# Low parts of every second piece of the output weights and last gate weights formed by an accumulating DMA instead of VectorE

## The chip, the cores and the metric

The kernel runs on one core of a Trainium2 chip. The metric is device time in microseconds (us) of one execution, from the start to the end of the program on that core. The engines of the core are TensorE (PE, with its weight loads PEld), VectorE (DVE), ScalarE (ACT), GpSimd (POOL) and SyncE (SP); each runs its own instructions in order and waits on semaphores of the others. DMA transfers are issued from the queues of SP, ACT and POOL and move data on 16 DMA engines that they share.

## What is computed

One block of a network over 256 rows of 2048 columns, in float32. The reference, cut to its frame:

```python
def reference(x, p, ...):
    h = x
    for l in range(DEPTH):                       # DEPTH is 1
        hn = rms_norm(h, ln_gain[l])
        z = split_columns(hn @ w_in[l] + b_in[l])
        y_a = rglru_branch(...) * silu(z['lru_gate'])
        y_b = nsa_branch(...) * silu(z['nsa_gate'])
        y_c = fox_branch(...) * silu(z['fox_gate'])
        mg = sigmoid(z['merge']).reshape(b, s, N_BRANCH, D_MODEL)
        merged = (mg[:, :, 0] * (y_a @ w_branch[l, 0])
                  + mg[:, :, 1] * (y_b @ w_branch[l, 1])
                  + mg[:, :, 2] * (y_c @ w_branch[l, 2]))
        h = h + merged @ w_out[l]                # "out"
        e = rms_norm(p[l] @ w_ple[l], ple_gain[l])
        h = h + sigmoid(h @ w_ple_gate[l]) * e   # "gate"
    return h
```

The change touches only the two last products, `merged @ w_out` and `h @ w_ple_gate`, each 256 x 2048 by 2048 x 2048.

## The kernel before

Every product is formed three times. An operand is cut into a high part, its rounding to float32r (a type that TensorE multiplies faster than float32), and a low part, the rest. With `hi`, `lo` of the activations and `wh`, `wl` of the weights, `mm3` adds hi x wh, hi x wl and lo x wh in PSUM.

All weights lie in one stream in HBM, in the order in which they are used, cut into 384 pieces. `plan()` lists the pieces. A full piece holds 128 rows x 1024 values, 512 KB. The stream ends with four chunks of kind "out" (512 columns each, 8 pieces each), three of kind "gate" (512 columns, 8 pieces each) and two of kind "gate" with 256 columns (4 pieces each): 64 pieces. I call the pieces of the second out chunk o1.0 to o1.7 (the chunks are o0 to o3), those of the gate chunks g0.0 and so on (g0 to g4). For each 512-column piece of these, `by_rows` issues 12 matmuls on PE: two row tiles, two blocks of 128 weight rows, three products; the first of a piece reads `wh`, the second `wl`.

The main loop is at piece i when it emits, in this order: the load of piece i + 5 on SP's queue (`issue`, tile `raw`, 4 buffers), the cut of piece i + 3 (`cut`), then what a new chunk needs (`before`), then the matmuls of piece i, then the end of the chunk, if it is its last piece. `cut` takes buffers `wh` and `wl` of rings of four. ACT writes `wh` as a copy of `raw` rounded to float32r, and DVE writes `wl = raw - wh`. As the ring has four buffers, `wh` of a piece waits until PE is through with the piece four places before.

`before` loads 512 KB from POOL's queue at the start of a chunk: `xc` (columns of x, for an out chunk) or `ec` (for a gate chunk, then also the 256 KB of `bias`, one buffer). Both `xc` and `ec` are tiles of the pool `k4`, a ring of five buffers of 4 KB a partition. DVE adds `xc` at the end of an out chunk (`k_h<-main,k_xc`); at the end of a gate chunk ACT takes a tanh of the sums (`k_fin<-main`), DVE multiplies it with `ec` (`k_fin<-k_fin,k_ec`) and adds h, and SP's queue stores it. After each out chunk the h just formed is turned by PE in two groups of four transposes (`bank<-cst,k_h`) among the first pieces of the next chunk. Side work beside the stream is over by the out chunks. Every operation passes a helper, so the profile gives one line, L191, for all of them.

Of the kernel before, what the change touches and what calls it, by code (L numbers as in the profile page):

```python
# [16 lines left out]
P = 128  # L17
# [5 lines left out]
EPS = 1e-6  # L23
# [17 lines left out]
# The small vectors, one column of 128 rows each.  # L41
# [8 lines left out]
# Constants of the shapes alone.  # L50
# [9 lines left out]
# Columns of the input projection whose products come out with rows on partitions, by chunk.  # L60
# [15 lines left out]
def plan():  # L76
    """The order of the weights: pieces of products, with what each needs and starts."""
# [53 lines left out]
    for c0, n in ((0, 512), (512, 512), (1024, 512), (1536, 256), (1792, 256)):  # L131
        out += item("gate", (c0, n), KT, n, ("w_ple_gate", None, [(c0, n)]), rows=1024 // n,
                    needs=lambda k: (f"ht{k // 4}",))
    at = 0
# [6 lines left out]
class Clock:  # L141
    """Estimates, in ns, of when each engine is through with what was emitted for it: an instruction
    starts once its engine is free and the last uses of its operands that matter to it are over."""
# [6 lines left out]
    def add(self, which, cost, out, ins, late=0.0):  # L150
        start = self.t[which]
        regions = [(out, True)] + [(x, False) for x in ins]
        spans = []
        for ap, writes in regions:
            free = list(ap.ap)[1:]
            lo = ap.offset
            hi = lo + sum(s * (n - 1) for s, n in free)
            name = ap.tensor.name
            # Two engines take turns at a bank of PSUM, whatever they do there.
            bank = name.startswith(("bank", "main"))  # L160
            if bank:
                lo, hi = 0, 1 << 30
            spans.append((name, lo, hi, writes))
            for l, h, t, w, e in self.uses.get(name, ()):
                if (writes or w or bank and e != which) and l <= hi and lo <= h:
                    start = max(start, t + (0.0 if e == which else 60.0))
        end = start + cost
        self.t[which] = end
        low = min(self.t[x] for x in ("pe", "v", "a"))
        for name, lo, hi, writes in spans:  # L170
            kept = [u for u in self.uses.get(name, ()) if u[2] > low and (bank or not writes or u[0] < lo or u[1] > hi)]
            self.uses[name] = kept + [(lo, hi, end + late, writes, which)]
# [8 lines left out]
class Metered:  # L181
    """An engine whose work is added to the clock."""
# [37 lines left out]
class Side:  # L220
    """Work beside the stream of weights, cut into steps that are dealt out along it."""
# [17 lines left out]
    def tick(self, hurry=False):  # L239
        """One step of every task that is under way, as long as the engines keep up."""  # L240
        while len(self.active) < self.most and self.pending:
            self.active.append(self.pending.popleft())
        for group in (self.urgent, self.active):
            for task in list(group):
                if self.clock.behind() > LIMITS[group is self.active] and not hurry:
                    return
                try:
                    if next(task[1]) and group is self.active:
                        group.remove(task)
                        group.append(task)  # L250
                except StopIteration:
                    self.done.add(task[0])
                    group.remove(task)
# [4 lines left out]
    def take(self, n=1):  # L258
        """n banks that are through with what was last in them."""
        while True:  # L260
            ready = [x for x in self.free if x[1] <= self.clock.t["pe"]]
            if len(ready) >= n:
                for x in ready[:n]:
                    self.free.remove(x)
                return [x[0] for x in ready[:n]]
            yield False
# [4 lines left out]
    def settle(self):  # L271
        """Until a product that reads what was emitted so far needn't wait for it."""
        t = self.clock.done()
        yield True
        while self.clock.t["pe"] < t:
            yield False

    def room(self, **need):
        """Room for a task's tiles."""
        while any(self.rooms[k] < n for k, n in need.items()):  # L280
            yield False
        self.give(**{k: -n for k, n in need.items()})
# [11 lines left out]
def block_kernel(ctx: ExitStack, tc: tile.TileContext, io):  # L294
# [44 lines left out]
    def splits(*parts):  # L339
        """Each source (times a scale) as the exact sum of two float32r tensors."""  # L340
# [16 lines left out]
    # ------------------------------------------------------------------ the stream of weights  # L357
# [4 lines left out]
    def issue(h, k=0, nk=None):  # L362
        """Loads a half's rows of 128, or nk of them from the k-th."""
# [7 lines left out]
    def cut(h, k=0, nk=None):  # L371
        m, n = h["nk"] * h["n"], h["n"]
        nk = nk or h["nk"]
        if k == 0:
            h["whl"] = [wp.tile([P, 1024], R32, tag=x, bufs=AHEAD + 1, name=nm(x)) for x in ("wh", "wl")]
        wh, wl = h["whl"]
        ks = slice(k * n, (k + nk) * n)
        split(wh[:, ks], wl[:, ks], h["raw"][:, ks])
# [5 lines left out]
    def by_rows(h, x):  # L384
        """Rows on partitions: two main banks, one of each row tile, gather the chunk's products."""
# [14 lines left out]
    def by_cols(h, x):  # L400
        """Columns on partitions: the chunk's column tiles in halves of main banks."""
# [14 lines left out]
    def banks_of(h):  # L416
        """The main banks of by_cols, each with its (first column tile, number of them)."""
# [7 lines left out]
    # ------------------------------------------------------------------ loads and constants  # L425
# [18 lines left out]
    # The causal mask of a tile, with none before and after.  # L444
# [13 lines left out]
    # Products of constants until the first weights are in: the array's clock rises with use.  # L458
# [3 lines left out]
    def rsqrt(out, ss, n):  # L462
        """out = (ss / n + EPS) ** -0.5"""
# [4 lines left out]
    def softplus(out, x, n):  # L468
        """out = max(x, 0) + log1p(exp(-|x|)), with log1p(u) = 2 atanh(u / (2 + u))"""
# [14 lines left out]
    def squares(x, acc, first):  # L484
        """acc += x^2, of two tiles"""
# [7 lines left out]
    def row_scales(name, acc):  # L493
        """(mean square of each of the 256 columns + EPS) ** -0.5, the same on all partitions."""
# [18 lines left out]
    # ------------------------------------------------------------------ operands kept on chip  # L513
# [13 lines left out]
    def hn_first(i, ks=range(2)):  # L527
        """Two tiles of x times its gain, as operands; the rows' scales come later."""
# [9 lines left out]
    def hn_again(i):  # L538
        """The same with the rows' scales."""
# [14 lines left out]
    # ---- p @ w_ple, normed, with its gain halved for the last gate  # L554
# [28 lines left out]
    # ---- gates: half of z (1 + tanh(z / 2)) is z sigmoid(z)  # L583
# [11 lines left out]
    # ---- RG-LRU, two tiles of 128 channels at a time  # L595
    def lru_task(i):
# [43 lines left out]
        # 1 - a^2 = tanh(-log a) (1 + a^2)  # L640
# [12 lines left out]
    # ---- keys and values of the sparse attention  # L653
    def unscaled(banks, dst, name, k0):
        """A chunk of the products without the rows' scales."""
# [9 lines left out]
    def cmp_task(banks):  # L665
        """The windows of 32 rows, with their positions added: 15 columns for each row and head."""
# [19 lines left out]
    def cmp_end():  # L686
# [6 lines left out]
        # The products with both parts of each block, added and turned.  # L693
# [31 lines left out]
    def norm_rows(z, n, dst):  # L725
        """dst(t) = z's groups of 128 columns, each row of a group normed."""
# [15 lines left out]
    def kk_task(z):  # L742
        # Of each head: window keys of row tiles 1 and 0, compressed keys, selected keys of tiles 0 and 1.
# [21 lines left out]
    # ---- sparse attention of a pair of heads and one row tile  # L765
    def nsa_task(g, pr, t):
# [18 lines left out]
        def soft(a, sc):  # L785
            """exp(score - maximum) and their sums: compressed, selected, window."""
# [71 lines left out]
    # ---- forgetting attention  # L858
    def forget_task():
# [10 lines left out]
        # lf holds softplus(-f) = -log f: the running sum is minus the cumulative log forget gate.  # L870
# [10 lines left out]
    def fox_task(h):  # L881
# [42 lines left out]
        # Key tile 0 of both row tiles, then key tile 1 of the second.  # L924
# [17 lines left out]
    # ---- branch outputs as operands  # L942
# [24 lines left out]
    def split_turned(name, dst, src, j, scale=None):  # L967
        """Columns 512 j .. of src, turned and split into dst."""
# [15 lines left out]
    # ------------------------------------------------------------------ the ends of chunks  # L984
# [49 lines left out]
    def read_by(name, gen):  # L1034
        """A task that reads the chunk's main banks."""
# [30 lines left out]
    def proj_chunk(h, out):  # L1066
        """merged += projection (1 + tanh): twice the gated sum, halved when it is split."""
# [33 lines left out]
    def before(h):  # L1101
        """What the end of a chunk asks for, loaded while its products are formed."""
# [14 lines left out]
    # ------------------------------------------------------------------ the program  # L1117
# [103 lines left out]
# The weights in flight; how many pieces are loaded and cut ahead.  # L1221
RAW, LOADS, AHEAD = 4, 5, 3
# Products of constants before the first weights.
WARM = 8
# Tiles of the pools that the tasks beside the stream may hold, and how many of them run at once.
ROOMS = dict(k1=7, k2=8, k4=5)
MOST = 3
# Nanoseconds: spared between an operand and its product; work that may wait on VectorE and ScalarE.
MARGIN = 1600.0
LIMITS = 3000.0, 2000.0  # L1230
# The first of p's products follows this chunk of the merge.
# [3 lines left out]
def stream(arrays):  # L1235
    """The weights, laid out one after the other as they are used."""
# [68 lines left out]
```

## Time and profile before

| | |
|---|---|
| median of three runs | 1110.47 us (1108.59 to 1111.84) |
| span of the profiled execution, first to last instruction | 1108.5 us |
| own time of the profiled execution | not listed apart; the lowest run stands 0.09 us above its span |
| PE busy | 1098.8 us, 99% of the span |
| DVE, ACT, POOL busy | 65%, 53%, 5% |
| moved by DMA | 220.88 MB, mean 199 GB/s |

Busy shares are means over the whole program. What a wait costs is read in the stretch in which it stands: the out and gate chunks fill the last 190 us or so of the span. Matmuls are pipelined, so one lasts longer in the profile (0.39 us) than the distance from it to the next (0.23 us).

### The profile page before, as it was taken

What the parts mean: (1) busy time and instruction counts of PE and PEld (TensorE: products, weight loads), DVE (VectorE), ACT (ScalarE), POOL (GpSimd) and SP (SyncE); (2) the same over time, 40 slices, a digit from 0 to 9 for tenths busy, and PEclk for the clock granted to TensorE, in tenths of its full rate; (3) what the DMA queues carried; (4) which work ended last, traced back from release to release, by engine and by line L of the source; (5) the groups of instructions that cost most, each with busy time, mean ns of one, the idle gap of its engine ahead of it and who ended that gap; (6) DMA issues with size and microseconds to landing.
All of it is one profiled execution on the core that took longest, in us unless ns stands there. A gap on an engine that the chain in (4) does not pass through costs nothing.

```text
span 1108.5 us, 16051 instructions
## 1 busy us (share of the span) xinstructions
PE 1098.8 (99%) x6123; PEld 957.4 (86%) x6123; DVE 725.9 (65%) x1108; ACT 588.2 (53%) x869; POOL 51.0 (5%) x70
## 2 busy tenths in 40 slices
PE   8999999999999999999999999999999999999998
PEld 8999998789988888888888888889888888888888
DVE  7679878877674765676776755554665565555554
ACT  7456786587654655454644544454554444444442
POOL 0100000010000000011010000000000100000000
PEclk9999999999999999999999999999999999999999
DMA  8656658756464554567557566766575775655773
GB/s 303 219 186 187 212 179 267 257 182 195 156 208 148 172 170 138 172 203 212 175 177 218 167 196 202 218 193 217 171 216 195 237 279 195 208 190 180 226 244 101
DMA packets 63293, 220.88 MB, mean 199 GB/s; under 512 B 7400, under 2 KB 8304, under 8 KB 63216
## 3 DMA queue, kind: packets, MB, share of 16 engines
q1 hardware_dynamic: 58176, 203.71, 55.6%
q0 software_dynamic: 4752, 15.76, 5.5%
q8 instruction: 48, 0.79, 0.3%
q10 hardware_dynamic: 288, 0.39, 0.1%
q14 instruction: 29, 0.24, 0.1%
HBM read 215.62 MB, written 4.20 MB: 198 GB/s over the span
## 4 chain that ended last, share of the span: by engine, by line
PE 97%; DMA 1%; DVE 1%; ACT 1%; issue 0%; DVEq 0%; ACTq 0%
PE main L191 90%; PE bank L191 7%; DMA raw<-in_w 1%; DVE wl L191 1%; ACT wh L191 0%; DMA k_xT<-in_xT 0%; ACT L191 0%; DVE k_fin L191 0%; DVE k_z L191 0%; ACT k_lru L191 0%; ACT k_hnh L191 0%; ACT k_fin L191 0%; DVEq L191 0%; ACTq L191 0%
## 5 line engine op out<-in xcount | busy, mean ns | idle before, releaser
L191 DVE TENSOR_TENSOR wl<-raw,wh 128x1024 fp32r<-128x1024 f32 (+3 forms) x385 | 463.8, 1211 | 320.2 <-ACT wh L191 319.1
L191 ACT ACTIVATE wh<-raw 128x1024 fp32r<-128x1024 f32 (+3 forms) x385 | 401.2, 1048 | 376.2 <-PE main L191 297.3
L191 PE MATMUL main<-wh,k_hnh 128*128 128x512 f32 (+1 forms) x736 | 285.0, 387 | 0.9 <-ACT wh L191 0.9
L191 PE MATMUL main<-wl,k_hnh 128*128 128x512 f32 (+1 forms) x736 | 281.3, 382 | 1.2 <-DVE wl L191 1.1
L191 PE MATMUL main<-wh,k_hnl 128*128 128x512 f32 (+1 forms) x736 | 281.0, 382 | 0.0
L191 PE MATMUL main<-k_hnh,wh 128*128 128x256 f32 x576 | 164.7, 286 | 1.5 <-ACT wh L191 1.5
L191 PE MATMUL main<-k_hnh,wl 128*128 128x256 f32 x576 | 164.1, 285 | 0.2 <-DVE wl L191 0.2
L191 PE MATMUL main<-k_hnl,wh 128*128 128x256 f32 x576 | 164.0, 285 | 0.0
L191 PEld LDWEIGHTS main<-wl,k_hnh 128*128 128x128 f32 x736 | 138.5, 188 | 26.7 <-DVE wl L191 2.6
L191 PEld LDWEIGHTS main<-wh,k_hnl 128*128 128x128 f32 x736 | 138.2, 188 | 26.7
L191 PEld LDWEIGHTS main<-wh,k_hnh 128*128 128x128 f32 x736 | 138.4, 188 | 26.3 <-ACT wh L191 1.2
L191 PEld LDWEIGHTS main<-k_hnh,wh 128*128 128x128 f32 x576 | 111.3, 193 | 2.0 <-ACT wh L191 1.8
L191 PEld LDWEIGHTS main<-k_hnh,wl 128*128 128x128 f32 x576 | 111.3, 193 | 0.5 <-DVE wl L191 0.4
L191 PEld LDWEIGHTS main<-k_hnl,wh 128*128 128x128 f32 x576 | 111.4, 193 | 0.1
L191 PE MATMUL main<-wh,k_yh 128*128 128x512 f32 x192 | 75.3, 392 | 0.0
L191 PE MATMUL main<-wh,k_yl 128*128 128x512 f32 x192 | 74.9, 390 | 0.0
L191 PE MATMUL main<-wl,k_yh 128*128 128x512 f32 x192 | 74.9, 390 | 0.0
L191 PE MATMUL main<-wh,k_hth 128*128 128x512 f32 (+1 forms) x160 | 55.7, 348 | 0.0
L191 PE MATMUL main<-wh,k_htl 128*128 128x512 f32 (+1 forms) x160 | 55.6, 347 | 0.0
L191 PE MATMUL main<-wl,k_hth 128*128 128x512 f32 (+1 forms) x160 | 55.5, 347 | 0.0
L191 PE MATMUL main<-wh,k_mth 128*128 128x512 f32 x128 | 50.7, 396 | 0.0
L191 PE MATMUL main<-wh,k_mtl 128*128 128x512 f32 x128 | 50.0, 391 | 0.0
(253 smaller groups left out, 1173.9 us busy)
## 6 DMA issues: line engine op xcount, KB each, us to landing
raw<-in_w SPq DMA_DIRECT2D x371, 512.0 KB, 4.1
bias<-in_b_in POOLq DMA_DIRECT2D x21, 256.0 KB, 4.3
raw<-in_w SPq DMA_DIRECT2D x8, 408.0 KB, 5.4
e_dram<-k_e POOLq DMA_DIRECT2D x4, 512.0 KB, 7.0
k_xc<-in_x POOLq DMA_DIRECT2D x4, 512.0 KB, 8.7
k_xT<-in_xT SPq DMA_DIRECT2D x7, 256.0 KB, 5.8
k_ec<-e_dram POOLq DMA_DIRECT2D x3, 512.0 KB, 7.8
out<-k_fin SPq DMA_DIRECT2D x6, 256.0 KB, 2.2
```

The lines of the kernel that those rows point to most:

```text
L191: r = call(out, *args, **kw)
```

## The change

Among the 64 pieces of the out and gate chunks every second one, from the 9th up to the 55th, is marked `summed`: pieces .0, .2, .4 and .6 of the chunks o1, o2, o3, g0, g1 and g2, 24 in all. For these the low part is formed otherwise. ACT writes the negated rounded weights into a tile `ws`, then a DMA from POOL's queue reads the same weights from HBM a second time and adds them to what stands in `ws`, so that `ws` holds weight minus high part. ACT then writes `wh` as before. DVE has nothing to do for these pieces. `ws` is not taken from the ring of `wl` but from the pool `k4`, which so far held `xc` and `ec` there.

```diff
@@ plan @@
+    last = [h for h in out if h["kind"] in ("out", "gate")]
+    for h in last[8:-8:2]:
+        h["summed"] = True
...
@@ cut @@
         if k == 0:
-            h["whl"] = [wp.tile([P, 1024], R32, tag=x, bufs=AHEAD + 1, name=nm(x)) for x in ("wh", "wl")]
+            h["whl"] = [wp.tile([P, 1024], R32, tag=x, bufs=AHEAD + 1, name=nm(x)) if x == "wh" or not h.get("summed")
+                        else mid([P, 1024], R32, name="ws") for x in ("wh", "wl")]
         wh, wl = h["whl"]
         ks = slice(k * n, (k + nk) * n)
-        split(wh[:, ks], wl[:, ks], h["raw"][:, ks])
+        if h.get("summed"):
+
+            A.activation(wl, h["raw"], AF.Copy, scale=-1.0)
+            G.dma_start(wl, bass.AP(tensor=wsrc.tensor, offset=wsrc.offset + h["off"], ap=[[m, P], [1, m]]),
+                        accum_op=OP.add)
+            A.activation(wh, h["raw"], AF.Copy)
+        else:
+            split(wh[:, ks], wl[:, ks], h["raw"][:, ks])
```

The rest of the diff takes comments out. The rows of PE and SP stand in the same order as before, but that PE reads `k_ws` in place of `wl`.

POOL's queue around the end of chunk g0 and the start of g1, before; a row is a DMA, written tile left of the arrow, `k_ec_9353` and `k_ec_9525` are the `ec` of g0 and g1:

```order
L191 DMA k_xc_9193<-in_x 128x2x512
L191 DMA k_ec_9353<-e_dram 128x2x512
L191 DMA bias_9355<-in_gain 128x512
L191 DMA k_ec_9525<-e_dram 128x2x512
L191 DMA bias_9527<-in_gain 128x512
```

The same place after the change; `k_ec_9367` and `k_ec_9543` are now the `ec` of g0 and g1:

```order
L194 DMA k_ec_9367<-e_dram 128x2x512
L194 DMA bias_9369<-in_gain 128x512
L194 DMA k_ws_9390<-in_w 128x1024
L194 DMA k_ws_9437<-in_w 128x1024
L194 DMA k_ws_9474<-in_w 128x1024
L194 DMA k_ws_9511<-in_w 128x1024
L194 DMA k_ec_9543<-e_dram 128x2x512
L194 DMA bias_9545<-in_gain 128x512
L194 DMA k_ws_9562<-in_w 128x1024
L194 DMA k_ws_9601<-in_w 128x1024
```

Between the `ec` of two chunks there are now four accumulating DMAs, so five tiles of `k4` after the `ec` of g0 comes that of g1, and takes its buffer. `k_ws_9562` is that of piece g1.4; it stands behind `ec` and `bias` of g1.

ACT at the same place before, from the end of g0; `wh_9521`, `wh_9543` and `wh_9561` are the high parts of g1.3, g1.4 and g1.5:

```order
L191 ACTIVATE k_fin_9509<-main_85 128x512
L191 ACTIVATE k_fin_9514<-main_86 128x512
L191 ACTIVATE wh_9521<-raw_9473 128x1024
L191 ACTIVATE wh_9543<-raw_9491 128x1024
L191 ACTIVATE wh_9561<-raw_9519 128x1024
```

ACT there after the change:

```order
L194 ACTIVATE k_fin_9527<-main_85 128x512
L194 ACTIVATE k_fin_9532<-main_86 128x512
L194 ACTIVATE wh_9539<-raw_9490 128x1024
L194 ACTIVATE k_ws_9562<-raw_9508 128x1024
L194 ACTIVATE wh_9561<-raw_9508 128x1024
L194 ACTIVATE wh_9580<-raw_9537 128x1024
L194 ACTIVATE k_ws_9601<-raw_9559 128x1024
```

The negated copy of g1.4, `k_ws_9562`, stands between the high parts of g1.3 and g1.4. It waits for no buffer of its own, but it stands behind `wh_9539`, which waits for PE.

## Rows read from the trace of the kernel before

**Rows 1.** The page, parts 1 and 4: busy time by engine, and the chain that ended last.

```profile
PE 1098.8 (99%) x6123; PEld 957.4 (86%) x6123; DVE 725.9 (65%) x1108; ACT 588.2 (53%) x869; POOL 51.0 (5%) x70
...
PE 97%; DMA 1%; DVE 1%; ACT 1%; issue 0%; DVEq 0%; ACTq 0%
```

**Rows 2.** The chain from 900 us on: start, duration, what.

```profile
972.33 0.44 PE bank L191 x4
...
975.54 0.44 PE bank L191 x4
...
1021.42 82.91 PE main L191 x456
1104.33 0.02 issue
1104.35 0.39 ACT k_fin L191
```

**Rows 3.** Groups of instructions from 880 us on: busy, mean ns, idle before.

```profile
L191 DVE TENSOR_TENSOR wl<-raw,wh 128x1024 fp32r<-128x1024 f32 x77 | 94.2, 1225 | 89.0 <-ACT wh L191 88.9
L191 ACT ACTIVATE wh<-raw 128x1024 fp32r<-128x1024 f32 x77 | 81.6, 1060 | 112.9 <-PE main L191 93.7 <-DMA raw<-in_w 18.6 <-ACT wh L191 0.7
```

**Rows 4.** Timeline of PE, one piece of o1: start, duration, instruction.

```profile
961.28 0.39 PE L191 MATMUL main<-wh,k_mth 128*128 128x512 f32 x1
961.51 0.39 PE L191 MATMUL main<-wl,k_mth 128*128 128x512 f32 x1
...
964.00 0.39 PE L191 MATMUL main<-wh,k_mth 128*128 128x512 f32 x1
```

**Rows 5.** Timeline of ACT: middle of o1, start of o2, start of g1.

```profile
961.48 1.06 ACT L191 ACTIVATE wh<-raw 128x1024 fp32r<-128x1024 f32 x1 [1.66 <-PE main L191]
...
969.64 1.06 ACT L191 ACTIVATE wh<-raw 128x1024 fp32r<-128x1024 f32 x1 [1.66 <-PE main L191]
...
1037.80 0.60 ACT L191 ACTIVATE k_fin<-main 128x512 f32<-128x512 f32 x1 [0.76 <-PE main L191]
1038.30 1.05 ACT L191 ACTIVATE wh<-raw 128x1024 fp32r<-128x1024 f32 x1
...
1046.22 1.06 ACT L191 ACTIVATE wh<-raw 128x1024 fp32r<-128x1024 f32 x1 [0.21 <-DMA raw<-in_w]
```

**Rows 6.** Timeline of DVE: end of o0, end of o1, end of g0.

```profile
948.02 1.23 DVE L191 TENSOR_TENSOR wl<-raw,wh 128x1024 fp32r<-128x1024 f32 x1 [0.30 <-ACT wh L191]
...
969.16 1.28 DVE L191 TENSOR_TENSOR k_h<-main,k_xc 128x512 f32<-128x512 f32 x2
...
1038.64 0.69 DVE L191 SCALAR_TENSOR_TENSOR k_fin<-k_fin,k_ec 128x512 f32<-128x512 f32 x1
```

**Rows 7.** Timeline of POOL: its DMAs from 881 us on.

```profile
881.35 2.85 POOL L191 DMA_DIRECT2D k_xc<-in_x  x4
884.20 0.70 POOL L191 DMA_DIRECT2D k_ec<-e_dram  x1
914.41 0.58 POOL L191 DMA_DIRECT2D bias<-in_gain  x1 [29.51 <-DVE k_mg L191]
948.02 0.71 POOL L191 DMA_DIRECT2D k_ec<-e_dram  x1 [33.03 <-DVE k_h L191]
```

**Rows 8.** Issue to landing: the k_ec of 948.02, the k_xc of 881.35, the k_ec of 884.20.

```profile
DMA to landing us min/median/max: 5.5/5.5/5.5
...
DMA to landing us min/median/max: 5.9/5.9/5.9
...
DMA to landing us min/median/max: 13.4/13.4/13.4
```

**Rows 9.** Issue to landing of raw, 940 to 1020 us (28 loads).

```profile
DMA to landing us min/median/max: 3.0/3.2/5.5
```

**Rows 10.** Stretches: busy time by engine, PEclk, DMA share, GB/s.

```profile
992.00:1015.00 23.00, 23.00 (x107) 19.05 (x106) 12.48 (x13) 9.46 (x10) 0.00 (x0) 1.00 0.54 184
1037.00:1060.00 23.00, 23.00 (x103) 19.07 (x102) 14.74 (x17) 10.06 (x12) 1.28 (x2) 1.00 0.69 229
```

**Rows 11.** GB/s from 880 to 1108.5 us in 40 slices of 5.71 us.

```profile
GB/s 217 354 404 269 188 199 224 209 165 180 201 206 268 162 199 202 211 136 204 212 192 147 211 192 194 143 278 112 268 290 319 73 263 253 318 122 255 69 3 46
```

## The prediction

> **What bounds the kernel now.** I read the page first: PE is busy for 99% of the span, and the chain that ended last runs on PE for 97% of it [rows 1]. Then I looked at the stretch that the change touches. The chain from 900 us on is PE alone: after the last group of transposes it is one run of 456 matmuls, 82.91 us, down to the first tanh after the last product [rows 2]. No wait of PE for `wl` or `wh` stands in it. PE takes a piece of 12 matmuls every 2.72 us (961.28 to 964.00), and reads `wl` in the second of them, 0.23 us into the piece [rows 4]. DVE and ACT are the ones that wait: DVE was idle for 89.0 us before its 77 subtractions, ACT for 112.9 us before its 77 copies, mostly for PE [rows 3]. The reader should see that what is taken from DVE here is taken from an engine that nobody waits for, and that the only thing the change can touch is the moment at which a low part is there.
>
> **What it removes and adds.** DVE loses 24 subtractions of 1.225 us, 29.4 us of work [rows 3]; worth nothing, since PE waited for none. ACT gains 24 copies of the same shape as `wh`, 1.06 us each, 25.4 us; in the out chunks it is busy 9.46 of 23.00 us [rows 10], and a pair of pieces (5.44 us) would hold three copies, 3.2 us. Hidden by the waits for PE; if they were gone it would cost as much as it lasts. POOL issues 24 DMAs of some 0.7 us [rows 7]; it does nothing else but six `xc` and `ec` and their biases. The raw buffer of a summed piece comes free at the end of ACT's copy and not of DVE's subtraction, some 1.2 us earlier, so SP's loads lose nothing by it. What remains is the transfer: 24 x 512 KB more from HBM, and as much read from SBUF to be added to.
>
> **The time that the transfer has, in the middle of a chunk.** Call S the start of piece j - 4 on PE. `wh` of j - 1 waits for the end of piece j - 5 and starts 0.20 us after S (961.48 against 961.28) [rows 4, 5]. It takes 1.06, the negated copy of j behind it 1.06: done at S + 2.32. PE wants `ws` at S + 4 x 2.72 + 0.23 = S + 11.11. So 8.8 us are left from issue to landing.
>
> **What the transfer takes.** The trace has no accumulating DMA, so I bound it. Below: a plain 512 KB from POOL's queue beside raw loads, 5.5 us [rows 8]. Above: the last of five such in a row, 13.4 us [rows 8]. The row of five also gives a pace: the first, issued at 881.35, landed 5.9 later, at 887.2; the fifth, issued at 884.20, at 897.6 [rows 7, 8]. That is 2.6 us for each further 512 KB when POOL's queue and SP's are both loaded. I count the accumulating one as two such shares, since it must fetch its target as well as its source: 5.5 + 2.6 = 8.1 us alone, and 5.2 behind another. I choose that over one share (it only copies) and over three because a second stream of the same size is the least that an addition in place needs. 8.1 is inside 8.8, and 5.2 inside the 5.44 of a pair, both narrowly: in the middle of a chunk I count no stall.
>
> The Trainium skill speaks here ("Collectives: The Full Stack", section "The bandwidth ceiling: the fold count and why AG ≠ RS ≠ AR"): an addition inside a DMA needs two source reads on the same ring and so runs at half the rate of a copy, measured as 62.28 against 32.35 GB/s. That would be 1.93 shares in place of two; by it the sum below would be some 8.3 us in place of 10.5 (0.36 less at each of six starts), and by the plain row alone nothing. No run here shows it.
>
> **At the start of a chunk** the transfer stands behind others. Now S is the start of the chunk on PE. The `ws` of piece .2 was issued at S - 5.44 + 2.32 and lands at S + 5.0. Behind it comes `xc` or `ec`, which now waits for the buffer of the chunk before: five tiles of `k4` earlier is the tile of that chunk. Before, all four `xc` and the first `ec` were issued by 884.9 [rows 7]. For o2, S is 969.44 (0.20 before the `wh` at 969.64), and DVE is through with `xc` at 970.44, S + 1.0 [rows 5, 6]. `xc` lands one share behind `ws`, at S + 7.6, and the `ws` of piece .4 two shares later, at S + 12.8. It is wanted at S + 11.11 + 0.88 (two groups of transposes [rows 2]) = S + 11.99. Late by 0.8 us; three times (o1, o2, o3), 2.4 us. For g1, S is 1037.60 (0.20 before the tanh at 1037.80), and DVE is through with `ec` at 1039.33, S + 1.7 [rows 5, 6]. `ec` lands at S + 7.6, 256 KB of `bias` at S + 8.9, the `ws` of g1.4 at S + 14.1; wanted at S + 11.11. Late by 3.0 us; g1 and g2, 6.0 us. g0 has the transposes too: 14.1 against 11.99, 2.1 us. What is late next: the `ws` of g1.6. In the trace of before the load of its `raw` came in at 1046.2 [rows 5], so its issue is at S + 9.7; it lands at S + 14.1 + 5.2 = 19.3, wanted at S + 16.55 + 3.0 = 19.55. In time. The DVE work that waits for `ec` holds back no low part that is needed before S + 16. Sum: 2.4 + 6.0 + 2.1 = **10.5 us**.
>
> The profile's span is 1108.5, the lowest run 0.1 above it; taking that as its own time, the sum is 1108.6 + 10.5 = 1119.1 for such an execution. The median of the runs stands 1.9 higher, and I give the time against it: 1110.47 + 10.5 = **1121.0 us**.
>
> **Rivals.** *In time everywhere (no change).* If the accumulating DMA costs what a copy does, it lands 5.5 us after its issue; at the start of g1 that is ec S + 7.2, bias S + 8.5, `ws` S + 11.1 against 11.11. PE never waits, and the time is 1110.5. For it: POOL's `ec` of 948.02 landed in 5.5 with raw loads beside it [rows 8], and the DMA engines are at 0.54 to 0.69 of their time here [rows 10]. Against: the target has to be read. It decides as soon as an accumulation costs under about half a share more. This is also the side on which nothing slower is seen; below it there is only the spread of the runs, since PE has no wait to lose.
>
> *DMA becomes the bound.* If an addition costs three shares, a pair of pieces moves five times 512 KB. The fullest slice of the trace moved 404 GB/s [rows 11], so 512 KB takes 1.30 us at best and the pair 6.5 against 5.44: 1.06 x 24 = 25 us, and six `xc` and `ec` with three biases another 7.5 x 1.30 = 9.8. Time 1145. For it: even with two shares the pair needs 5.2 of 5.44, so little is left; raw loads beside a full POOL queue would become late as well. Against: raw loads land in 3.2 us in the median [rows 9].
>
> *POOL held up by DVE.* If a subtraction on DVE kept POOL from issuing, each issue could come 1.2 us later: 8.1 + 1.2 = 9.3 against 8.8, 0.5 us for each of six transfers in mid-chunk, and 1.2 at each of six starts: 10.2 more, 1131. Against: the `ec` issued at 948.02 stood beside a subtraction that started at the same moment and took 1.23 us; the issue took 0.71, and its landing, 5.5, is the shortest of that size [rows 6 to 8]. The Trainium skill ("SBUF — State Buffer", section "Who interferes with whom") says that a DVE operation with two inputs in SBUF contends with GpSimd's reads, and one in a two-port mode locks GpSimd out altogether. By that row, the trace does not show it for this pair.
>
> **How the numbers follow.** Late at the starts of chunks, as summed: 0.45. In time everywhere: 0.26. DMA the bound: 0.25. POOL held up: 0.04. A measurement of this kernel tells some 0.3%, 3.3 us, from no change. The first, third and fourth are slower; the second is "same", but for 0.03 of luck below. A little of the first ends under 3.3 us, which gives faster 0.03, same 0.25, slower 0.72. The range reaches from the case in time, 1109.5, to just past the case in which DMA is the bound, 1146; the likeliest case's own range is 1114 to 1131 (an accumulation of 1.7 to 2.3 shares).
>
> **What would show it.** Of the changed kernel: a wait of PE for the DMA of `k_ws`, longest at the second matmul of g1.4 and g2.4 (about 3 us), under 1 us in the out chunks, none for `wh`; the landing of `k_ws` at 8 us in the middle of a chunk and 9 to 11 at its start; `ec` of g1 issued at 1.7 us after the chunk's start; DVE 29 us less busy, ACT 25 more. Landings of 5.5 to 7 would make the second case right, landings over 10 everywhere with raw loads late too the third. The prediction is wrong if PE waits in mid-chunk, or if nothing waits.

## The result and the profile after

The changed kernel takes 1125.04 us in the median of 4 runs (1122.58 to 1126.09), the kernel before 1110.18 us beside it: 14.9 us more, ratio 1.013 with a 95% interval of 1.0116 to 1.0144. The forecast was 1121.0, slower. The profiled execution has a span of 1123.1 us, 14.6 more than before.

The page of the changed kernel, part 1, then parts 3 and 6 in three rows (DMA queues with packets, MB, share of 16 engines; issues with KB each and us to landing):

```profile
PE 1105.4 (98%) x6123; PEld 960.5 (86%) x6123; DVE 698.3 (62%) x1084; ACT 611.7 (54%) x893; POOL 70.9 (6%) x94
...
q0 software_dynamic: 8208, 28.34, 11.3%
...
k_ws<-in_w POOLq DMA_DIRECT2D x24, 512.0 KB, 8.5
```

Against [rows 1], DVE is busy for 27.6 us less and ACT for 23.5 us more: the work went where the change sends it, and the end came later all the same.

The waits of PE from 930 us on (in total, times, longest); before, there was none [rows 2]:

```profile
PE main L194 <- DMA k_ws<-in_w: 8.9, 6, 3.8
```

Stretches of the changed kernel, one for each chunk o1, o2, o3, g0, g1, g2 from its first matmul to that of the next (columns as in [rows 10]: busy time by engine, PEclk, DMA share, GB/s):

```profile
946.24:969.98 23.74, 23.31 (x106) 18.67 (x104) 7.58 (x8) 13.36 (x14) 3.98 (x5) 1.00 1.02 292
969.98:993.10 23.12, 23.12 (x106) 18.61 (x104) 7.58 (x8) 13.47 (x14) 4.01 (x5) 1.00 1.00 291
993.10:1016.84 23.74, 23.32 (x105) 18.65 (x104) 7.58 (x8) 13.37 (x14) 4.55 (x6) 1.00 1.00 290
1016.84:1040.66 23.82, 23.35 (x105) 18.65 (x104) 8.83 (x10) 13.85 (x15) 4.63 (x6) 1.00 1.03 294
1040.66:1068.42 27.76, 23.83 (x98) 18.95 (x97) 8.85 (x11) 13.24 (x14) 4.60 (x6) 0.94 1.00 286
1068.42:1095.76 27.34, 23.53 (x98) 19.00 (x97) 10.86 (x13) 11.24 (x12) 3.65 (x5) 0.94 0.84 266
```

The second number is the length of the chunk. Before, the chunks o1 to g0 took 22.72 us each (the copies of `wh` that PE's end of a chunk released started at 946.92, 969.64, 992.36 and 1015.08) and g1 and g2 21.76. So the chunks are longer by 1.0, 0.4, 1.0, 1.1, 6.0 and 5.6 us, 15.1 in all, and three quarters of that lies in two of them. The other thing to see is the DMA share: 1.0, where it was 0.54 to 0.69 [rows 10], at under 300 GB/s, while the trace of before had a slice of 404 [rows 11]; only g2, with its long wait, has less, 0.84. In g1 and g2 the granted clock of PE is also lower.

The waits of PE in the out chunks and g0; the chunks o1, o3 and g0 start at 946.24, 993.10 and 1016.84:

```profile
958.88 0.50 PE L194 MATMUL main<-k_ws,k_mth 128*128 128x512 f32 x1 [0.43 <-DMA k_ws<-in_w]
993.88 0.50 PE L194 MATMUL main<-k_ws,k_mth 128*128 128x512 f32 x1 [0.40 <-DMA k_ws<-in_w]
1017.58 0.50 PE L194 MATMUL main<-k_ws,k_hth 128*128 128x512 f32 x1 [0.35 <-DMA k_ws<-in_w]
```

By their distance from the start of the chunk these are the second matmuls of o1.4, o3.0 and g0.0, each 0.5 to 0.6 us late.

The two stretches of g1 after its long wait, and PE's rows there:

```profile
1061.50:1066.00 4.50, 4.41 (x13) 3.52 (x14) 0.00 (x0) 1.11 (x2) 2.02 (x3) 0.64 1.05 289
1066.00:1080.00 14.00, 14.00 (x64) 11.58 (x63) 3.89 (x6) 6.29 (x8) 0.88 (x1) 1.00 0.95 276
```

```profile
1051.54 0.39 PE L194 MATMUL main<-wh,k_hth 128*128 128x512 f32 x1
1053.00 0.50 PE L194 MATMUL main<-k_ws,k_hth 128*128 128x512 f32 x1 [1.07 <-DMA k_ws<-in_w]
...
1061.60 0.80 PE L194 MATMUL main<-k_ws,k_hth 128*128 128x512 f32 x1 [2.86 <-DMA k_ws<-in_w]
1062.19 0.63 PE L194 MATMUL main<-wh,k_htl 128*128 128x512 f32 x1
1062.62 0.63 PE L194 MATMUL main<-wh,k_hth 128*128 128x512 f32 x1
```

The two that waited are the second matmuls of g1.4 and g1.6. The first came 1.2 us later than its place in the row (1053.00 against 1051.54 + 0.23), the other 3.0 us. After it the matmuls stand 0.43 us apart in place of 0.23 for six of them. In g2 nothing waits at g2.4, and g2.6 is late by 4.0 us:

```profile
1088.94 0.79 PE L194 MATMUL main<-k_ws,k_hth 128*128 128x512 f32 x1 [3.81 <-DMA k_ws<-in_w]
```

Why g1.6? The timeline of ACT in g1, and of POOL:

```profile
1050.65 1.06 ACT L194 ACTIVATE wh<-raw 128x1024 fp32r<-128x1024 f32 x1 [5.95 <-DMA raw<-in_w]
1053.53 1.06 ACT L194 ACTIVATE k_ws<-raw 128x1024 fp32r<-128x1024 f32 x1 [1.82 <-DMA raw<-in_w]
```

```profile
1037.73 0.84 POOL L194 DMA_DIRECT2D k_ws<-in_w  x1 [5.05 <-ACT k_ws L194]
1038.27 0.92 POOL L194 DMA_DIRECT2D k_ec<-e_dram  x1
1039.00 0.75 POOL L194 DMA_DIRECT2D bias<-in_gain  x1
1043.66 0.88 POOL L194 DMA_DIRECT2D k_ws<-in_w  x1 [3.91 <-ACT k_ws L194]
1054.89 0.86 POOL L194 DMA_DIRECT2D k_ws<-in_w  x1 [10.36 <-ACT k_ws L194]
```

ACT stood for 5.95 us before `wh` of g1.5 and 1.82 us before the negated copy of g1.6, both times for `raw`. On SP's queue the two stores of chunk g0 stand ahead of these loads:

```profile
1041.58 0.35 SPq L194 DMA_DIRECT2D out<-k_fin  x1
1042.94 0.34 SPq L194 DMA_DIRECT2D out<-k_fin  x1
1043.38 0.43 SPq L194 DMA_DIRECT2D raw<-in_w  x1
```

That order is the one of the kernel before, and the load of g1.5 starts no later in the chunk than it did (2.7 us after its start; 2.9 before). What grew is the time to landing: 7.2 us for g1.5, where it took 4.3, and 9.5 for g1.6, where it took 5.1. Before, ACT already waited at this place, without cost to PE:

```profile
1044.95 1.06 ACT L191 ACTIVATE wh<-raw 128x1024 fp32r<-128x1024 f32 x1 [3.37 <-DMA raw<-in_w]
```

So the accumulating DMA of g1.6 was issued at 1054.89, 14.2 us after the start of the chunk, and landed 6.7 us later, while PE wanted it at 1058.6. It was not this transfer that was slow, at 6.7 us against a median of 8.5, but its start that was late.

### The profile page after: what moved, and what is told of

The parts are those of the page before. It is cut to its first block, busy times and chain, and to the rows that moved or that the text cites. A ratio compares the mean times of both kernels' runs of the same rounds, so it can differ in the third digit from the quotient of the medians.

```text
span 1123.1 us, 16112 instructions
## 1 busy us (share of the span) xinstructions
PE 1105.4 (98%) x6123; PEld 960.5 (86%) x6123; DVE 698.3 (62%) x1084; ACT 611.7 (54%) x893; POOL 70.9 (6%) x94
## 4 chain that ended last, share of the span: by engine, by line
PE 86%; issue 6%; DMA 4%; ACT 1%; POOL 1%; DVE 1%; SPq 0%; POOLq 0%; ACTq 0%; DVEq 0%
PE main L194 80%; PE bank L194 6%; DMA k_ws<-in_w 3%; DMA raw<-in_w 1%; POOL k_ws L194 1%; ACT wh L194 1%; DVE wl L194 0%; ACT k_ws L194 0%; ACT k_lru L194 0%; ACT L194 0%; SPq L194 0%; POOL k_xc L194 0%; DVE k_lru L194 0%; DVE sp_nss L194 0%; DVE k_fin L194 0%
## 5 line engine op out<-in xcount | busy, mean ns | idle before, releaser
L194 DVE TENSOR_TENSOR wl<-raw,wh 128x1024 fp32r<-128x1024 f32 (+1 forms) x361 | 434.2, 1210 | 333.8 <-ACT wh L194 332.6
L194 PEld LDWEIGHTS main<-wh,k_yl 128*128 128x128 f32 x192 | 36.0, 188 | 7.6
```

The source lines that it names most:

```text
L194: r = call(out, *args, **kw)
```

## The experiments

Theory after the result: an addition takes more of the DMA engines than a copy, they are full, and then two things are late: `k_ws` itself, and `raw`, above all where its loads stand behind the stores. Rivals: PE's wait for `k_ws` is the whole loss; or the order within POOL's queue is; or the second read from HBM costs as such. Each run stands beside runs of the kernel before with medians of 1110.03 to 1110.15 us.

**Copy in place of the addition.**

```diff
-            G.dma_start(wl, bass.AP(...), accum_op=OP.add)
+            G.dma_start(wl, bass.AP(...))
```

> The DMA of the 24 summed pieces copies the weights instead of adding them, so the low part of these pieces is the whole weight; all else as in the changed kernel. Theory (the addition costs a second share of DMA time, since it reads its target too): the landing of k_ws falls from 8.5 to about 6 us, the loads of raw land in under 5 us, and the time to 1110 to 1114. Rival (the second read of 512 KB from HBM and the wait for it are the cost, the addition nothing): landing stays at 8 us or more and the time above 1120.

1114.07 us, ratio 1.0046 (1.0027 to 1.0065): 4.0 us over before, at the edge of its range, where the addition costs 14.9. The DMA rows of this kernel, and then of the changed one, each over its chunks o1 to g2 (946 to 1084 us, 946 to 1096 us):

```profile
q1 hardware_dynamic: 7389, 25.82, 52.3%
q0 software_dynamic: 4624, 16.65, 36.3%
...
raw<-in_w SPq DMA_DIRECT2D x46, 512.0 KB, 6.4
k_ws<-in_w POOLq DMA_DIRECT2D x22, 512.0 KB, 5.6
```

```profile
q0 software_dynamic: 4624, 16.65, 51.1%
q1 hardware_dynamic: 7449, 26.06, 46.3%
...
raw<-in_w SPq DMA_DIRECT2D x46, 512.0 KB, 7.8
k_ws<-in_w POOLq DMA_DIRECT2D x22, 512.0 KB, 8.5
```

The same 16.65 MB in POOL's queue take 36.3% of 138 us, 50.1 us of all engines, as copies, and 51.1% of 150 us, 76.7 us, with 22 additions: 1.2 us more for each. 512 KB take 50.1 / 31.8 = 1.58 us as a copy, so an addition takes 2.8, or 1.76 of a copy, in the mean over the queue. SP's loads (q1) are a control: 512 KB of them take 1.5 us beside copies and 1.4 beside additions, so fuller engines do not by themselves make the figure larger. The records of single packets say it more directly: over the chunks o1 to g1 the median one of 4 KB in POOL's queue took 0.33 us in the changed kernel and 0.17 us here, a ratio of 1.9. An addition lands 2.9 us later than a copy. `raw` landed later than the 5 us expected even beside copies.

**Stores two pieces later.**

```diff
-            Q.dma_start(io["out"][:, t, c0:c0 + n], s)
+            late.append((n_now[0] + 2, io["out"][:, t, c0:c0 + n], s))
...
+        while late and late[0][0] <= i:
+            _, dst, src = late.pop(0)
+            Q.dma_start(dst, src)
```

> The two stores of a gate chunk are put on SP's queue two pieces later, so that the loads of raw for g1.5, g1.6, g2.5 and g2.6 no longer stand behind them. Theory (in g1 and g2 raw lands late behind the stores, so the negated copy of piece .6 is late and PE waits 3 to 4 us for it): the chunks g1 and g2 lose 2 us or less each against before instead of 6.0 and 5.6, no wait of over 2 us is left, time 1115 to 1118. Rival (the transfer of k_ws stands behind ec and bias in POOL's queue): 1123 to 1126, the waits stay.

1118.47 us, ratio 1.0066 (1.0048 to 1.0084): 6.6 us off the changed kernel. g1 is now 1.5 us longer than before and g2 2.4, where 2 or less was expected. PE's waits fall to this:

```profile
PE main L194 <- DMA k_ws<-in_w: 4.4, 6, 1.2
```

The wait of 3.8 us is gone, as the theory says; the time came out just above its range.

**The same stores on the kernel before.**

> The kernel before with the two stores of a gate chunk put on SP's queue two pieces later, nothing else. If the gain of the later stores (6.6 us on the changed kernel) comes only from raw being late under the added traffic: 1109 to 1111, no gain. If the stores cost the kernel before something as well: below 1108.

1109.93 us, ratio 0.9999 (0.9990 to 1.0008). The order of stores and loads costs the kernel before nothing that shows, at its DMA share of 0.54 to 0.69 [rows 10]; in the changed kernel, at 1.0, it costs 6.6 us.

**All the work done, the sum read by nobody.**

```diff
         if h.get("summed"):
-            A.activation(wl, h["raw"], AF.Copy, scale=-1.0)
-            G.dma_start(wl, bass.AP(...),
+            ws = mid([P, 1024], R32, name="ws")
+            A.activation(ws, h["raw"], AF.Copy, scale=-1.0)
+            G.dma_start(ws, bass.AP(...),
                         accum_op=OP.add)
-            A.activation(wh, h["raw"], AF.Copy)
-        else:
+        if True:
             split(wh[:, ks], wl[:, ks], h["raw"][:, ks])
```

> All that the change adds is done (negated copy on ACT, accumulating DMA, the tile of k4), but PE reads the low part that DVE forms as before; the sum in k_ws is read by nobody. Theory (the loss is the waiting of PE for k_ws alone): 1110 to 1112, with the same slow landings of raw. Rival (the added traffic makes raw so late that PE waits for wh and wl as well): 1115 or more, with waits of PE for ACT or DVE in g1 and g2.

1119.43 us, ratio 1.0075 (1.0047 to 1.0103). The rival was right: some 9.4 us of the 14.9 (by the interval 5 to 11) are there although PE waits for no sum. PE waits for what comes from `raw`, which landed after 8.1 us in the median:

```profile
PE main L194 <- ACT wh L194: 4.3, 2, 4.1
PE main L194 <- DVE wl L194: 2.2, 4, 0.8
```

**Sum read by nobody, stores two pieces later.** Both edits above.

> The added work with its sum read by nobody (as in the run in which only the traffic stays), and the stores two pieces later. Theory (the traffic costs time only where the loads of raw also start late behind the stores): 1110 to 1112, no wait of PE over 0.5 us. Rival (the engines are simply full, wherever the loads start): 1116 to 1119.

1112.51 us, ratio 1.0021 (1.0011 to 1.0031). The DMA engines are as full as in the changed kernel (three stretches of this run, the last two over g1 and most of g2):

```profile
970.00:1037.00 67.00, 67.00 (x308) 55.47 (x307) 37.09 (x38) 39.15 (x41) 11.16 (x14) 1.00 1.03 302
1037.00:1060.00 23.00, 23.00 (x103) 19.05 (x102) 12.34 (x14) 12.35 (x15) 4.60 (x6) 1.00 1.03 308
1060.00:1083.00 23.00, 22.23 (x97) 17.85 (x96) 12.29 (x13) 10.44 (x12) 5.68 (x8) 1.00 1.01 295
```

Yet only 2.4 us are lost, just above the range. Two waits stand there, both over the 0.5 us expected:

```profile
PE main L194 <- DVE wl L194: 1.6, 2, 0.9
```

A DMA share of 1.03 alone does not stop PE: from 1037 to 1083 us the loads of `raw` even land after 9.7 us in the median, but they start earlier and arrive in time. They cost when they also start late.

The four runs make a square:

| us over the kernel before | stores as they were | two pieces later | difference |
|---|---|---|---|
| PE reads the sum | 14.9 | 8.4 | 6.5 |
| nobody reads it | 9.4 | 2.4 | 7.0 |
| difference | 5.5 | 6.0 | |

Within the noise the two effects add up: about 6.7 us for loads behind the stores, 5.7 for waiting for the sum, 2.4 for the rest. The intervals of the four times are 1.6, 2.0, 3.1 and 1.1 us to either side (by rows), so the two effects are known to some 2 us each and the rest to 1, and which of the two is the larger stays open.

**Copy and later stores.**

> The 24 DMAs copy the weights instead of adding them (the low part of these pieces is the whole weight), and the stores of the gate chunks stand two pieces later on SP's queue. Theory (the loss is made of the second share of an addition, and of raw late behind the stores): 1109 to 1112, no wait of PE over 0.5 us. Rival (the second read from HBM has a cost of its own that neither explains): 1113 or more.

1110.52 us, ratio 1.0006 (0.9997 to 1.0015), no wait of PE. The second read of the weights from HBM, 12.6 MB, and ACT's 24 further copies show no cost by themselves; the interval allows 1.7 us at most.

**`xc`, `ec` and `bias` behind the addition of piece .4.**

```diff
-        if kind in ("rows", "out", "gate") and h["nth"] == (2 if kind == "rows" else 0):
+        if kind in ("rows", "out", "gate") and h["nth"] == (2 if kind == "rows" else 1):
```

> The loads of xc, ec and bias are issued one piece later, so that they stand behind the accumulating DMA of piece .4 in POOL's queue and no longer ahead of it. Theory of the prediction (the transfer of piece .4 is late because these are ahead of it): the waits at o2.4, o3.4 and g1.4 (0.4 to 1.2 us) go, time 1121 to 1123; those at g1.6 and g2.6 stay. Rival (the DMA engines are full and the order within POOL's queue does not matter): 1124 to 1126.

1124.93 us, ratio 1.0125 (1.0104 to 1.0146). No gain: the order in POOL's queue, on which the prediction built its waits, only moves them. Counted from the starts of the chunks in this trace, the wait at g1.4 stayed (0.94 us; 1.07 in the changed kernel), although `ec` and `bias` no longer stood ahead of it, one of 1.66 us came at g2.4, and the longest is again at g1.6. I had also misread where the small waits of the changed kernel stood: at o1.4, o3.0 and g0.0, and not at o2.4 and o3.4.

```profile
PE main L194 <- DMA k_ws<-in_w: 10.7, 6, 5.0
```

**Every fourth piece, and the same with later stores.** `last[8:-8:4]` in place of `last[8:-8:2]`.

> Only every fourth piece is summed (pieces .0 and .4 of the six chunks, 12 in all); all else as in the changed kernel. Theory (the accumulating DMAs fill the DMA engines, so that raw and k_ws are both late): with half of them the engines have room, raw lands in about 4 us, PE waits under 1 us in all, time 1110 to 1113. Rival (each chunk start costs its own wait, since piece .4 is still there): 1113 to 1118, with the waits at piece .4.

> Every fourth piece summed (12 in all), stores two pieces later. Theory (with half the additions the engines have room, and what was left of 4.2 us came from raw and k_ws behind the stores and their chunk's ec): 1109 to 1112. Rival (the additions at the start of a chunk cost their wait whatever the stores do): 1113 or more, with the waits at piece .4 of g1 and g2.

1114.31 us, ratio 1.0040 (1.0025 to 1.0055), and 1111.92 us, ratio 1.0012 (1.0001 to 1.0022). Half the additions cost 4.2 us. My 1110 to 1113 was too low; the time lies in the rival's range, and one of two waits stands where the rival put it. These are the waits of the first run:

```profile
PE main L194 <- DMA k_ws<-in_w: 2.8, 2, 1.7
```

The wait of 1.7 us is at g1.4, whose addition was issued in time, at 1040.84, and landed after 10.0 us; that of 1.1 is at g2.0, whose `raw` was late. With the stores later 1.8 us are left, inside the theory's range, and a single wait, 0.9 us at g2.4. By the medians, what is late behind the stores makes 2.4 of the 4.2 us.

**Only the out chunks.** `last[8:32:2]`.

> Only the pieces of the out chunks o1, o2 and o3 are summed (12 of 24). From the lengths of the chunks in the changed kernel (1.0, 0.4 and 1.0 us longer than before): 1112 to 1114. Rival (the loss stands wherever DMA is full, and moves with it): 1115 or more.

1111.03 us, ratio 1.0009 (1.0000 to 1.0018): 0.9 us for 12 additions, below its range and less than the 2.4 us by which these chunks were longer in the changed kernel's trace. There are no stores among them, and there the additions nearly fit.

**The addition one piece earlier, stores two later.** The negated copy and its DMA are emitted for piece i + 4 ahead of the cut of i + 3.

> Stores two pieces later, and the negated copy and its DMA one piece earlier (2.72 us). Theory (what is left after the later stores, 8 us, is k_ws landing at 8 to 10 us against 8.8): the waits for k_ws go, time 1110 to 1113. Rival (the engines are full, and an earlier start only lets raw be later): 1115 to 1119, with waits for wh or wl.

1128.36 us, ratio 1.0166 (1.0126 to 1.0206): 9.9 us more than with the later stores alone. Against the change itself the intervals overlap. ACT works in order, and the earlier copy stands waiting for a `raw` that is not there, with the `wh` of the next pieces behind it. Three of its rows:

```profile
987.12 1.06 ACT L194 ACTIVATE k_ws<-raw 128x1024 fp32r<-128x1024 f32 x1 [8.46 <-DMA raw<-in_w]
...
1015.74 1.06 ACT L194 ACTIVATE k_ws<-raw 128x1024 fp32r<-128x1024 f32 x1 [9.81 <-DMA raw<-in_w]
...
1071.31 1.06 ACT L194 ACTIVATE k_ws<-raw 128x1024 fp32r<-128x1024 f32 x1 [8.28 <-DMA raw<-in_w]
```

The rival's outcome, though worse than its range, and by another way than it said: the waits of PE for `k_ws` did not go, they grew from 4.4 us with the later stores alone (the trace is that of the slowest of the four runs, 1134.5 us):

```profile
PE main L194 <- DMA k_ws<-in_w: 12.6, 8, 4.1
```

None of these kernels is faster than the kernel before.

## Why the prediction was right, and where it was off

**The time was right, the places of the waits were not.** The prediction named its own signs: PE waits longest at g1.4 and g2.4, about 3 us each, and it is wrong if PE waits in mid-chunk. The trace has 1.2 us at g1.4, nothing at g2.4, and the longest waits, 3.0 and 4.0 us, at g1.6 and g2.6, where no stall was counted. A term that was too large and one that was put at nothing made up for each other in part. That the time came out 4 us above the forecast, inside the range, is so far luck.

**DVE's work is worth nothing: right.** 27.6 us less on DVE bought no time, since PE had waited for none of it.

**An addition counts two shares: nearly right.** Measured 1.76 of a copy in engine time, 1.9 by the median packet; it landed after 8.5 us in the median where I had 8.1, a copy after 5.6 where I had 5.5. The 1.93 of the Trainium skill ("Collectives: The Full Stack", section "The bandwidth ceiling: the fold count and why AG ≠ RS ≠ AR") is the ratio of two collectives, one that copies and one that adds. This trace agrees with it in kind, from somewhat below.

**The out chunks: right in size, not in place.** 2.4 us forecast, as 0.8 at each of o1.4, o2.4 and o3.4; 2.4 in the trace (0.9 when they were alone), with waits at o1.4 and o3.0 and none at o2.4 and o3.4. For g0 I had 2.1, at g0.4, and 1.1 came, the larger part at g0.0.

**"It now waits for the buffer of the chunk before": wrong, but without weight in the sum.** `ec` of g1 was issued at 1038.27, right behind the addition of g1.2 and 2.4 us before the chunk began. Five tiles later is not the same buffer: in the built program `ec` of g1 lies where the `ws` of g0.4 had lain, which PE had finished some 6 us earlier. In the sum the wait ended 1.7 us into the chunk, ahead of the landing of that addition at 5.0, so nothing hung on it.

**3.0 us at g1.4: too large.** The four transfers ahead of and at g1.4, in order, with us from issue to landing (issued at 1037.73, 1038.27, 1039.00 and 1043.66):

```profile
k_ws<-in_w POOLq DMA_DIRECT2D x1, 512.0 KB, 6.4
k_ec<-e_dram POOLq DMA_DIRECT2D x1, 512.0 KB, 7.8
bias<-in_gain POOLq DMA_DIRECT2D x1, 256.0 KB, 8.3
k_ws<-in_w POOLq DMA_DIRECT2D x1, 512.0 KB, 9.3
```

They landed 3.5, 5.4, 6.6 and 12.3 us into the chunk, where I had 5.0, 7.6, 8.9 and 14.1. The first came earlier, and `ec` stood 1.9 behind it in place of 2.6. So g1.4 was late by 1.2 us.

**"SP's loads lose nothing by it", and "In time" for g1.6: wrong, and the largest miss.** I looked at when SP may issue the loads and not at how long they take once the engines are full, nor at the two stores ahead of them. ACT's wait of 3.37 us for `raw` of g1.5 stood in the trace of before and was a sign of it. From 880 us on the loads land after 7.1 us in the median, where 3.2 was the median in the stretch of [rows 9]. The addition of g1.6 was issued 14.2 us after the start of the chunk; I had taken its `raw` from the trace of before, which gave 9.7. The term for g1 and g2 was 6.0 us and measured 11.6: 1.2 at g1.4, 3.0 at g1.6, 4.0 at g2.6, and some 3.2 from PE's lower clock after the two long waits (granted 0.64 over 4.5 us, 0.61 over 4.1), which I had left out.

**The third rival was partly true.** The engines were full in five of the six chunks, as it said, and the loads of `raw` were late. But full engines alone cost 2.4 us, not 35: with the later stores and no reader the same transfers fitted. What I did not have is that the loss is a sum of PE waiting for the sum and of `raw` late behind stores that had cost nothing before, each some 6 us.

What stays open: the 2.4 us that are left with both removed (waits of 0.8 and 0.9 us for `wl` in g2 and after it show part of them), and why the addition of g1.4 still came late with `ec` and `bias` behind it.

## What to carry to other kernels

Work taken from an engine that nobody waits for buys nothing, and the transfer that replaces it takes from a resource that everybody uses: look at what else lands later. When DMA engines go from 60% to full, an order on a queue that was harmless can begin to cost; here it was stores ahead of loads. A wait that an engine has for free before the change shows where. Starting a dependent transfer earlier on an engine that works in order can block what stands behind it.

## What the runs showed of the hardware

An accumulating DMA of 512 KB into SBUF held the 16 engines for 2.8 us against 1.58 for a copy. The bytes shown are the same for both, 16.65 MB, so the rate shown falls: 290 GB/s at a DMA share of 1.0. POOL's issue of it took 0.83 to 0.92 us, that of the copy 0.53 to 0.56.

After waits of 3.0 and 4.0 us PE's granted clock was 0.64 and 0.61 over the next 4 us: matmuls 0.43 us apart, the level of 1.2 GHz, then 0.23 again, that of 2.4 GHz. After the wait of 1.2 us in g1 it did not fall.
